# A written TensorE order for the chunked scans, low halves on VectorE, and one offset for all matmul operands

## The chip, the cores and the metric

One core of one Trainium2 chip runs the whole program. The metric is device time of one execution in microseconds (us). The kernel before was timed three times: 1361.96, 1358.02 and 1358.82 us, median 1358.82. TensorE is called PE, VectorE DVE (in code `V`), ScalarE ACT (`A`), GpSimd POOL (`G`), and SP is the engine whose queue issues nearly all DMAs.

## What is computed

The reference is an encoder of two layers on x of shape (1, 512, 1024) in float32. Cut to its bones:

```python
for layer in (0, 1):
    if layer == 0:  # one input projection for both kinds of heads
        q, k, v, z, xbc, dt = split(rms_norm(x) @ w_in)
        a = neighbourhood_attention(rms_norm(q), rms_norm(k), v, rel_bias)   # 8 heads of 64
        xs, B, C = split(silu(conv4(xbc)))                                   # 16 heads of 64, 4 groups
        y = ssd_scan(xs, dt, B, C) + flip(ssd_scan(flipped)) + D * xs        # 4 chunks of 128 tokens
        x = x + concat(a, group_rms_norm(y * silu(z))) @ w_out               # 1536 -> 1024
    else:
        x = x + grouped_query_attention(rotary(rms_norm(x) @ w_qkv)) @ w_o
    g, u = split(rms_norm(x) @ w13)                                          # hidden 2816
    x = x + (silu(g) * u) @ w2
```

Within a chunk of the scan, `y = ((C B^T) * decay) (x dt)`; between chunks a state of 128 x 64 per head is passed on, forward and backward.

## The kernel before

Activations are kept transposed: eight tiles of 128 channels by 512 tokens. Every large product is formed from three matmuls in fp32r, because each operand is split in a high half (rounded to fp32r) and a low half (the rest): `mm3` (L139 to L144) issues low weights by high activations (L142), high by low (L143) and high by high (L144). `load_w` (L130 to L137) brings 128 x 1024 raw weights by a DMA on SP's queue (L134), ACT copies the high half (L135), and DVE or POOL subtracts to get the low half (L136). `prep` (L160) splits activations the same way (high L162, low L163).

A block of projections is a generator of eight steps, each one `mm3`, so 24 matmuls of 128x512. `stream` loads the weights of a block one block ahead. In layer 0, 32 steps of query and key blocks come first; then `run(n)` threads the rest of those blocks and the six blocks of scan group 0 between the parts of the attention heads (`quota`, L664); step 96 calls `dt_path`, which works out the time steps and their cumulated decays.

Then the loop at L689 goes over the four groups of the scan. It drains the stream of the group's six blocks `g{g}_{i}` (two gates, B, C and two x blocks, each of the last four with a convolution of three DVE operations, L507) and writes down `ssd_group(g)` (L538 to L660) as one piece. Its matmuls, in the order of the program: four transposes `bt` and eight `xt`, the products `cb` of B and C, the states `st` from `xw` (x times dt-weights; forward half on DVE, backward half on POOL, L566), then for two head pairs the products `yd` of `xtok` with the masked decays `cf` (worked out head by head by ACT, DVE and POOL, L597 to L625), and `yo` from the passed states `H` (L583, L586). Adding up, gating and a group norm (`gs`, L649 to L660) follow; the result is split into `so..xh`, `so..xl`. The tile scheduler decides how PE interleaves a group's small matmuls with the next group's projections; nothing in the code fixes it. The low halves of the weights of groups 1 to 3 and of the output projection (L703, 16 loads of 640 columns) are worked out by POOL. The output projection `oA` (L697 to L706) and the last two scan tiles' share (`tail`, bank `t`) end the mixer. The sum of squares for the norm of each FFN is added up on POOL (`sumsq`, L720; `f_acc`, L173), while DVE works out `f_xl` (L163).

PSUM banks are handed out by tag (`bank`, L81): `p` two and `x` one for projections, `s` two, `t` two, `c` one for the scan. SBUF tiles come from pools in the order in which they are opened; in the built program the weights, `xg`, `x` and `s` tiles start at byte addresses that are 480 modulo 512, and the tiles of the lanes opened by a layer's part (`early`, `mix`, `grp`, `n`, `nb`, the `hh`/`hl` of the FFN, the attention's tiles) at 448 modulo 512.

Of the kernel before, what the change touches and what calls it, by code (L numbers as in the profile page):

```python
# [37 lines left out]
W2_SPLIT = (8, 8, 6)  # L38
NSLOT = 12
PB, HLB = 6, 4  # L40
WARM = 10
# [23 lines left out]
def encoder_kernel(ctx: ExitStack, tc: tile.TileContext, xt, vec, cst, rope, nab, w_v, w_qk, w_dt, w_ssd,  # L65
# [38 lines left out]
    def f(ap):  # L104
        return ap.bitcast(F32)
# [24 lines left out]
    def load_w(src, cols, name, eng=None):  # L130
        hi = wsp.tile([P, 1024], F32R, name=f"{name}_h", tag="wh", bufs=WH)
        lo = wsp.tile([P, 1024], F32R, name=f"{name}_l", tag="wl", bufs=WL)
        raw = wsp.tile([P, 1024], F32, name=f"{name}_r", tag="wr", bufs=WR)[:, 0:cols]
        nc.sync.dma_start(raw, src)  # L134
        A.activation(hi[:, 0:cols], raw, AF.Copy)  # L135
        (eng or V).tensor_tensor(lo[:, 0:cols], raw, f(hi)[:, 0:cols], ALU.subtract)  # L136
        return hi, lo  # L137
# [69 lines left out]
    def even_mixer(lp):  # L207
# [5 lines left out]
        A.preload_act_table_set(LNEXP)  # L213
        zt = small("zt", P, 1)
        V.memset(zt, 0.0)
# [6 lines left out]
        for n in range(2):  # L222
            t = lp.tile([P, 6, S], F32R, name=f"early{n}", tag="grp", bufs=2)
            early += [t[:, i] for i in range(6)]
# [285 lines left out]
        def ssd_blocks(g):  # L510
            gt = lp.tile([P, 6, S], F32, name=f"grp{g}", tag="grp", bufs=2)
            conv_cols = (8 + g, 12 + g, 2 * g, 2 * g + 1)

            def matmuls(w, i):
                ps = bank(f"g{g}_{i}")
                for k in range(KB):
                    mm3(ps, w, k * P, xn[k], ALL, k == 0, k == KB - 1)
                    yield
                if i > 3:
                    A.activation(gt[:, i], ps, AF.Copy)  # L520
                else:
                    conv(ps, conv_cols[i], gt[:, i])
                if i == 3:
                    si = A.activation(gt, gt, AF.Silu)
# [13 lines left out]
        def ssd_group(g, gt):  # L538
# [7 lines left out]
            for i in range(2):  # L546
                ps = bank(f"xt{g}_{i}", "t")
# [3 lines left out]
                A.activation(t, ps, AF.Copy)  # L551
                xtok.append(t)
            ps = bank(f"cb{g}", "t")
            for c in range(NCH):
# [7 lines left out]
            for d in range(2):  # L562
                for i in range(2):
                    t = xslot(f"xw{g}_{d}_{i}")
                    h0 = d * 16 + g * RG + 2 * i
                    (V if d == 0 else G).tensor_tensor(t.rearrange("p (c h e) -> p c h e", c=NCH, h=2),  # L566
                                    xtok[i].rearrange("p (c h e) -> p c h e", c=NCH, h=2),
                                    d3v(wst)[:, :, h0:h0 + 2].unsqueeze(3).to_broadcast([P, NCH, 2, HD]), ALU.mult)
                    xw.append(t)
            H = lane(f"H{g}", "hs", 1, cols=3 * S).rearrange("p (n d h e) -> p n d h e", n=3, d=2, h=RG)  # L570
            for n in range(3):
                sps = bank(f"st{g}_{n}", "s")
                for d in range(2):
# [12 lines left out]
                V.tensor_tensor(H[:, n], H[:, n], s5, ALU.add)  # L586

            ys = []
            for i in range(2):
                yd = bank(f"yd{g}_{i}", "c")  # L590
                es = []
                for hh in range(2):
# [32 lines left out]
                    V.tensor_tensor(e, e, m, ALU.mult)  # L625
                    es.append(e)
                for c in range(NCH):
                    for hh, e in enumerate(es):
                        T.matmul(yd[64 * hh:64 * hh + 64, c * P:(c + 1) * P],
                                 xtok[i][:, c * P + hh * 64:c * P + hh * 64 + 64], e[:, c * P:(c + 1) * P],  # L630
                                 start=True, stop=True)
# [16 lines left out]
                ys.append(y)  # L648
            gs = bank(f"gs{g}", "s")  # L649
# [4 lines left out]
            sum_rows(gs, sqs[0], f"gs{g}")  # L654
            r = rsqrt_wide(gs, 1.0 / 256, f"gn{g}")
# [5 lines left out]

        blocks = [t for b in range(4) for t in qk_blocks(b)] + list(ssd_blocks(0))
        fill = stream(blocks, 1)
        quota = (12, 12, 10, 10, 8, 8, 6, 6, 6, 6)  # L664
        steps = [0]

        def run(n):
            for _ in range(n):
                next(fill, None)
                steps[0] += 1  # L670
                if steps[0] == 96:
                    dt_path()

        run(32)
        for i in range(10):
            n = quota[i]
            cuts = (0, (n + 2) // 3, (2 * n + 2) // 3, n)
# [19 lines left out]
        for k in range(KB):  # L697
            res[k] = xslot(f"xr{k}")
            nc.sync.dma_start(res[k], xt[k])
        for o in range(KB):  # L700
            ps = bank(f"oA{o}")
            for k, n in ((0, 5), (5, 5)):
                w = load_w(w_o0[o, :, k * P:(k + n) * P], n * P, f"wo{o}_{k}", G)  # L703
                for kk in range(n):
                    mm3(ps, w, kk * P, mix[k + kk], ALL, k + kk == 0, k + kk == 9)
            V.tensor_tensor(res[o], res[o], ps, ALU.add)  # L706
        tail(w_t0, mix[10:], "t0")
# [11 lines left out]

    def sumsq(name):  # L720
        acc = None
        for k in range(KB):
            acc = accsq(acc, res[k], name, G)
        return acc

    def ffn(layer, gname, hp):
# [9 lines left out]
        for i in range(HB):  # L736
# [429 lines left out]
```

## Time and profile before

| | us |
|---|---|
| median of three runs | 1358.82 |
| the profiled execution, its own time | 1357.06 |
| its span, first to last instruction | 1355.3 |
| PE busy in the span | 1311.6 |
| DVE busy | 806.6 |
| ACT busy | 606.4 |
| POOL busy | 267.4 |
| first matmul of group 0's states (`st`) | 169.2 |
| first matmul of FFN 0 | 401.1 |

The profiled execution is 1.76 us below the median. The mean granted clock of TensorE was 0.992 of full speed. Busy times of PE rest on modelled ends; the spacing of starts is what a row of equal matmuls really takes.

### The profile page before, as it was taken

The numbers are of one execution on the slowest core, as the hardware profiler recorded it, in microseconds if no ns is written. First come the engines' busy times: TensorE is split into PE (matmuls) and PEld (weight loads), VectorE is DVE, ScalarE is ACT, GpSimd is POOL, SyncE is SP. The second block draws the span as 40 slices with busy tenths as digits, with TensorE's granted clock in tenths as the row PEclk, the third lists the DMA queues.
The fourth block names the chain that finished last, engine by engine and source line by source line (L and its number), as shares of the span: only waits on it lengthen the run. The fifth ranks groups of instructions, "written<-read, shape, count | busy, mean of one in ns | idle before, by whom it ended". The sixth has DMA issues, their size and how long they took to land.

```text
span 1355.3 us, 16780 instructions
## 1 busy us (share of the span) xinstructions
PE 1311.6 (97%) x6278; PEld 1067.1 (79%) x6278; DVE 806.6 (60%) x1210; ACT 606.4 (45%) x1028; POOL 267.4 (20%) x240
## 2 busy tenths in 40 slices
PE   9999988989999999999999999999999999999998
PEld 7777776767777888888888878778878888888886
DVE  6788697887766444444323377998874444443221
ACT  6675566566444233222222347777653222332220
POOL 4013344343340000000000135655230000000000
PEclk9999999989999999999999999999999999999999
DMA  6344343434433332333333334321123233233331
GB/s 232 94 118 141 88 148 95 139 98 132 125 97 110 103 99 93 93 101 113 89 99 89 104 103 100 105 58 40 47 94 94 93 99 104 94 94 102 104 116 52
DMA packets 49761, 138.82 MB, mean 102 GB/s; under 512 B 6736, under 2 KB 6864, under 8 KB 49680
## 3 DMA queue, kind: packets, MB, share of 16 engines
q1 hardware_dynamic: 49392, 137.23, 33.3%
q8 instruction: 49, 0.80, 0.2%
q10 hardware_dynamic: 288, 0.52, 0.1%
q14 instruction: 32, 0.26, 0.1%
HBM read 127.11 MB, written 2.23 MB: 95 GB/s over the span
## 4 chain that ended last, share of the span: by engine, by line
PE 77%; DVE 14%; ACT 5%; issue 3%; DMA 1%; POOL 0%; SPq 0%; DVEq 0%; ACTq 0%; POOLq 0%
PE fo L144 6%; PE fo L142 6%; PE fo L143 6%; PE fu L144 6%; PE fu L142 6%; PE fu L143 6%; PE fg L143 6%; PE fg L144 6%; PE fg L142 6%; PE vps L260 2%; PE g L144 1%; PE g L142 1%; PE g L143 1%; PE opt L921 1%; DVE f_xl L163 1%
## 5 line engine op out<-in xcount | busy, mean ns | idle before, releaser
L143 PE MATMUL fg<-f_xl,wfg_h 128*128 128x512 f32 x352 | 137.1, 390 | 3.9 <-DVE f_xl L163 3.9
L142 PE MATMUL fo<-hh,wf_l 128*128 128x512 f32 x352 | 139.2, 396 | 0.0
L143 PE MATMUL fo<-hl,wf_h 128*128 128x512 f32 x352 | 139.2, 396 | 0.0
L144 PE MATMUL fo<-hh,wf_h 128*128 128x512 f32 x352 | 139.2, 396 | 0.0
L144 PE MATMUL fg<-f_xh,wfg_h 128*128 128x512 f32 x352 | 136.9, 389 | 0.0
L142 PE MATMUL fu<-f_xh,wfu_l 128*128 128x512 f32 x352 | 136.9, 389 | 0.0
L144 PE MATMUL fu<-f_xh,wfu_h 128*128 128x512 f32 x352 | 136.9, 389 | 0.0
L143 PE MATMUL fu<-f_xl,wfu_h 128*128 128x512 f32 x352 | 136.9, 389 | 0.0
L142 PE MATMUL fg<-f_xh,wfg_l 128*128 128x512 f32 x352 | 136.9, 389 | 0.0
L135 ACT ACTIVATE wf_h<-wf_r 128x1024 fp32r<-128x1024 f32 (+1 forms) x48 | 47.5, 989 | 186.5 <-PE fo L144 164.4
L136 DVE TENSOR_TENSOR wf_l<-wf_r,wf_h 128x1024 fp32r<-128x1024 f32 (+1 forms) x48 | 54.5, 1136 | 126.7 <-ACT wf_h L135 126.7
L135 ACT ACTIVATE wfg_h<-wfg_r 128x1024 fp32r<-128x1024 f32 x44 | 46.7, 1060 | 149.6 <-issue 131.2
L135 ACT ACTIVATE wfu_h<-wfu_r 128x1024 fp32r<-128x1024 f32 x44 | 46.7, 1061 | 130.6 <-PE fg L144 130.1
L745 DVE TENSOR_TENSOR g<-fu,fr_r 128x512 f32<-128x512 f32 x44 | 30.4, 691 | 124.3 <-PE fu L144 123.1
L743 DVE TENSOR_TENSOR g<-fg,fr_r 128x512 f32<-128x512 f32 x44 | 30.2, 691 | 88.2 <-PE fg L144 88.1
L143 PEld LDWEIGHTS fg<-f_xl,wfg_h 128*128 128x128 f32 x352 | 66.1, 188 | 18.6 <-DVE f_xl L163 4.8
L173 POOL TENSOR_TENSOR o_acc<-o_acc,o_sq 128x512 f32<-128x512 f32 x7 | 10.8, 1538 | 350.6 <-ACT o_sq L172 350.6
L144 PEld LDWEIGHTS fo<-hh,wf_h 128*128 128x128 f32 x352 | 66.1, 188 | 16.1
L143 PEld LDWEIGHTS fo<-hl,wf_h 128*128 128x128 f32 x352 | 66.1, 188 | 15.9
L142 PEld LDWEIGHTS fo<-hh,wf_l 128*128 128x128 f32 x352 | 66.1, 188 | 15.9
L142 PE MATMUL g<-n_xh,w_l 128*128 128x512 f32 x192 | 78.3, 408 | 0.0
L144 PE MATMUL g<-n_xh,w_h 128*128 128x512 f32 x192 | 78.1, 407 | 0.0
(415 smaller groups left out, 3153.6 us busy)
## 6 DMA issues: line engine op xcount, KB each, us to landing
wfg_r<-in_w_fa SPq DMA_DIRECT2D x44, 512.0 KB, 3.5
wfu_r<-in_w_fa SPq DMA_DIRECT2D x44, 512.0 KB, 3.5
wf_r<-in_w_fb SPq DMA_DIRECT2D x32, 512.0 KB, 3.5
w_r<-in_w_ssd SPq DMA_DIRECT2D x24, 512.0 KB, 3.6
wf_r<-in_w_fb SPq DMA_DIRECT2D x16, 384.0 KB, 3.1
wo_r<-in_w_o SPq DMA_DIRECT2D x16, 320.0 KB, 2.9
nb<-in_nab SPq DMA_DIRECT2D x16, 256.0 KB, 3.0
ec<-ecumd SPq DMA_DIRECT2D x32, 128.0 KB, 3.5
```

Source lines behind the costliest of these rows:

```text
L135: A.activation(hi[:, 0:cols], raw, AF.Copy)
L136: (eng or V).tensor_tensor(lo[:, 0:cols], raw, f(hi)[:, 0:cols], ALU.subtract)
L142: T.matmul(ps, wl[:, a], xh[:, b], start=first, stop=False)
L143: T.matmul(ps, wh[:, a], xl[:, b], start=False, stop=False)
L144: T.matmul(ps, wh[:, a], xh[:, b], start=False, stop=last)
L163: V.scalar_tensor_tensor(lo, xt, g, f(hi), ALU.mult, ALU.subtract)
L173: eng.tensor_tensor(acc, acc, sq, ALU.add)
L260: T.matmul(vps[t], x_, w_[:, ws_], start=k + n == 0, stop=k == KB - 1 and n == 2)
L743: V.tensor_tensor(g, gp, rstd, ALU.mult)
L745: V.tensor_tensor(g, up, rstd, ALU.mult)
L921: T.transpose(pt[:, a * 256 + n * P:a * 256 + (n + 1) * P], pr[n][:, (2 * kp + a) * P:(2 * kp + a + 1) * P], ident)
```

## The change

It has four parts.

**A written PE order.** Inside `tc.manual_schedule(engines={PE})` PE runs in program order. `ssd_group` becomes a generator that stops at five places, and between them `run` takes a fixed number of steps (`SSD_QUOTA`) out of one continuous stream: all projection blocks of all groups, and behind them the output projection. Each group starts `LEAD` steps behind the end of its own projections. The group norm is split off (`ssd_norm`) and runs `NORM_LAG` steps later. The output projection goes in trios of blocks: the eight k-blocks from attention and the first two groups for each block of the trio, then the next two k-blocks for all three. Banks of the scan move (`cb` from `t` to `s`, and so on) and `grp` has three buffers.

**Low halves off POOL.** All low halves of weights in the scan, the backward `xw` and the FFNs' sums of squares move to DVE. POOL keeps `mb` and `cb` of the heads.

**One offset.** A dummy tile of 544 bytes replaces `zt` (512 bytes) in the pool `sm`; all tiles of the layers' parts then start at 480 modulo 512, as the weights do.

**Room.** The DMA scratch shrinks from 16384 to 2048 bytes, which makes room for the third `grp`.

Line numbers shift: the matmuls of `mm3` are L153 to L155, the low half L147, `bt` L553, `xt` L560, `cb` L566, `xw` L577, `st` L589, `yd` L643, `yo` L656, `gs` L680 and L681.

```diff
+LEAD = (12, 12, 12, 0)
+SSD_QUOTA = ((10, 8, 10, 2, 12), (10, 8, 10, 2, 12), (10, 8, 10, 2, 12), (10, 8, 10, 2, 12))
+NORM_LAG = (12, 12, 6, 14)
+SHIFT = 136
...
+    V.memset(sm.tile([P, SHIFT], F32, name="shift", tag="shift", bufs=1)[:, 0:1], 0.0)
...
-        zt = small("zt", P, 1)
+        zt = lane("zt", "nb", 2)[:, 0:P]
...
-                yield (lambda i=i: load_w(w_ssd[g * 6 + i], 1024, f"w{g}_{i}", V if g == 0 else G)), lambda w, i=i: matmuls(w, i)
+                yield (lambda i=i: load_w(w_ssd[g * 6 + i], 1024, f"w{g}_{i}", V)), lambda w, i=i: matmuls(w, i)
...
-                    (V if d == 0 else G).tensor_tensor(t.rearrange("p (c h e) -> p c h e", c=NCH, h=2),
+                    V.tensor_tensor(t.rearrange("p (c h e) -> p c h e", c=NCH, h=2),
...
+        def out_blocks():
+            for trio in (range(3), range(3, 6), range(6, KB)):
+                ps = {}
+                for o in trio:
+                    ps[o] = bank(f"oA{o}")
+                    w = load_w(w_o0[o, :, 0:8 * P], 8 * P, f"wo{o}", V)
+                    for k in range(8):
+                        mm3(ps[o], w, k * P, (ctx_n + ssd_out)[k], ALL, k == 0, False)
+                        yield
+                w = load_w([w_o0[o, :, 8 * P:10 * P] for o in trio], 256 * len(trio), f"wq{trio[0]}", V)
...
+        def both():
+            yield from stream(blocks, 1)
+            yield from out_blocks()
...
-        for g in range(SSD_G):
-            if g:
-                fill = stream(list(ssd_blocks(g)), 1)
+        with tc.manual_schedule(engines={mybir.EngineType.PE}):
+            for g in range(SSD_G):
+                while steps[0] < 64 + 48 * (g + 1) + LEAD[g]:
+                    run(1)
+                for at in ssd_group(g, ready[g]):
+                    run(SSD_QUOTA[g][at])
+                norm = ssd_norm(g)
+                next(norm)
+                later.append((steps[0] + NORM_LAG[g], norm))
+            while later:
+                run(1)
             for _ in fill:
                 pass
-            ssd_group(g, ready[g])
...
-                rstd = bcast_rstd(sumsq(f"f{layer}"), f"fr{layer}")
+                rstd = bcast_rstd(sumsq(f"f{layer}", V), f"fr{layer}")
```

PE, at the start of group 0's scan, before (the number behind a letter and `_` is the group; `g1_5` is a projection of group 1, `cb0`, `st0` and `xw0` belong to the scan of group 0):

```order
L555 MATMUL cb0_1693<-grp0_390 128x128 x4
L577 MATMUL st0_0_1711<-xw0_0_0_1702,btok0_1677 128x128
L577 MATMUL st0_1_1717<-xw0_0_0_1702,btok0_1677 128x128
L142 MATMUL g1_5_1956<-n7_xh_945,w1_5_l_1919 128x512
L577 MATMUL st0_0_1711<-xw0_0_1_1704,btok0_1677 128x128
L577 MATMUL st0_0_1711<-xw0_1_0_1706,btok0_1677 128x128
L577 MATMUL st0_0_1711<-xw0_1_1_1708,btok0_1677 128x128
L577 MATMUL st0_1_1717<-xw0_0_1_1704,btok0_1677 128x128
L577 MATMUL st0_1_1717<-xw0_1_0_1706,btok0_1677 128x128
L577 MATMUL st0_1_1717<-xw0_1_1_1708,btok0_1677 128x128
L143 MATMUL g1_5_1956<-n7_xl_946,w1_5_h_1918 128x512
```

The states followed the products `cb0` at once, with single matmuls of the projection between them. The same place now, behind ten steps (30 matmuls) of `g1_5` and `g1_0` that follow `cb0`:

```order
L153 MATMUL g1_0_1793<-n5_xh_735,w1_0_l_1718 128x512
L154 MATMUL g1_0_1793<-n5_xl_736,w1_0_h_1717 128x512
L155 MATMUL g1_0_1793<-n5_xh_735,w1_0_h_1717 128x512
L589 MATMUL st0_0_1813<-xw0_0_0_1766,btok0_1741 128x128
L589 MATMUL st0_0_1813<-xw0_0_1_1768,btok0_1741 128x128
L589 MATMUL st0_0_1813<-xw0_1_0_1770,btok0_1741 128x128
L589 MATMUL st0_0_1813<-xw0_1_1_1772,btok0_1741 128x128
L589 MATMUL st0_1_1819<-xw0_0_0_1766,btok0_1741 128x128
L589 MATMUL st0_1_1819<-xw0_0_1_1768,btok0_1741 128x128
L589 MATMUL st0_1_1819<-xw0_1_0_1770,btok0_1741 128x128
L589 MATMUL st0_1_1819<-xw0_1_1_1772,btok0_1741 128x128
```

The twelve matmuls of the states stand in one piece, and 30 matmuls lie between `cb0` and them.

POOL, from the scan of group 0 on, before (`w1_2_l` is the low half of a weight of group 1, `w2_4_l` of group 2):

```order
L566 TENSOR_TENSOR xw0_1_0_1706<-xtok0_0_1684,wst_385 128x512
L566 TENSOR_TENSOR xw0_1_1_1708<-xtok0_1_1691,wst_385 128x512
L608 TENSOR_TENSOR cb1_1757<-cb1_1757,cum_383 128x512
L606 TENSOR_TENSOR mb2_1811<-cbg0_1699,dt_382 128x512
L136 TENSOR_TENSOR w1_2_l_2018<-w1_2_r_2019,w1_2_h_2017 128x1024
L606 TENSOR_TENSOR mb3_1833<-cbg0_1699,dt_382 128x512
L608 TENSOR_TENSOR cb3_1830<-cb3_1830,cum_383 128x512
L136 TENSOR_TENSOR w1_3_l_2053<-w1_3_r_2054,w1_3_h_2052 128x1024
```

The same engine now:

```order
L621 TENSOR_TENSOR cb1_1894<-cb1_1894,cum_385 128x512
L619 TENSOR_TENSOR mb2_2006<-cbg0_1763,dt_384 128x512
L621 TENSOR_TENSOR cb3_2025<-cb3_2025,cum_385 128x512
L619 TENSOR_TENSOR mb3_2028<-cbg0_1763,dt_384 128x512
L621 TENSOR_TENSOR cb5_2339<-cb5_2339,cum_385 128x512
L619 TENSOR_TENSOR mb6_2451<-cbg1_2183,dt_384 128x512
```

Only four operations per group (two `cb`, two `mb`) remain on POOL; the `xw` and the low halves stand in DVE's row instead.

More of the change, by code (lines that the diff above doesn't have):

```diff
@@ L133, in load_w @@
         raw = wsp.tile([P, 1024], F32, name=f"{name}_r", tag="wr", bufs=WR)[:, 0:cols]
-        nc.sync.dma_start(raw, src)
+        parts = src if isinstance(src, list) else [src]
+        for n, part in enumerate(parts):
+            w = cols // len(parts)
+            nc.sync.dma_start(raw[:, n * w:(n + 1) * w], part)
         A.activation(hi[:, 0:cols], raw, AF.Copy)
@@ L222, in even_mixer @@
         for n in range(2):
-            t = lp.tile([P, 6, S], F32R, name=f"early{n}", tag="grp", bufs=2)
+            t = lp.tile([P, 6, S], F32R, name=f"early{n}", tag="grp", bufs=3)
             early += [t[:, i] for i in range(6)]
@@ L626, in ssd_group @@
                     es.append(e)
+                yield 2 + 2 * i
                 for c in range(NCH):
@@ L648, in ssd_group, with ssd_norm @@
                 ys.append(y)
-            gs = bank(f"gs{g}", "s")
+                if i == 0:
+                    yield 3
+            ssd_y[g] = ys
+        ssd_y = {}
+        def ssd_norm(g):
+            ys = ssd_y[g]
             sqs = [slot(f"gsq{g}_{i}") for i in range(2)]
@@ L660, in ssd_group @@
                                           mixslot if g < 3 else xgslot)
[L662 to L665, printed above, removed]
+        def out_blocks():
[6 more added lines that the diff above has]
+                        mm3(ps[o], w, k * P, (ctx_n + ssd_out)[k], ALL, k == 0, False)
+                        yield
+                w = load_w([w_o0[o, :, 8 * P:10 * P] for o in trio], 256 * len(trio), f"wq{trio[0]}", V)
+                for n, o in enumerate(trio):
+                    res[o] = xslot(f"xr{o}")
+                    nc.sync.dma_start(res[o], xt[o])
+                    for k in range(2):
+                        mm3(ps[o], w, (2 * n + k) * P, ssd_out[4 + k], ALL, False, k == 1)
+                        yield
+                    V.tensor_tensor(res[o], res[o], ps[o], ALU.add)
+        blocks = [t for b in range(4) for t in qk_blocks(b)] + [t for g in range(SSD_G) for t in ssd_blocks(g)]
+        def both():
+            yield from stream(blocks, 1)
+            yield from out_blocks()
+        fill = both()
+        steps, later = [0], []
         def run(n):
@@ L670, in run @@
                 steps[0] += 1
-                if steps[0] == 96:
+                if steps[0] == DT_STEP:
                     dt_path()
+                if later and steps[0] >= later[0][0]:
+                    next(later.pop(0)[1], None)
         run(32)
         for i in range(10):
-            n = quota[i]
+            n = NA_QUOTA[i]
             cuts = (0, (n + 2) // 3, (2 * n + 2) // 3, n)
```

36 lines of the change are left out of this document (18 added, 18 removed).

## The prediction

> **What bounds the kernel now.** I read the page first, then the windows, the waits, and the groups of each engine for the stage that the change rewrites. The page's chain says who ends last:
>
> ```profile
> PE 77%; DVE 14%; ACT 5%; issue 3%; DMA 1%; POOL 0%; SPq 0%; DVEq 0%; ACTq 0%; POOLq 0%
> ```
>
> TensorE carries the kernel, so time can come from two places alone: from PE standing idle, and from matmuls that take longer than they need. The windows from group 0's states (169) to the first FFN matmul (401) show the first (columns: window, length, busy time and count of PE, weight loads, DVE, ACT, POOL, then granted clock, DMA share, GB/s):
>
> ```profile
> 169.00:224.00 55.00, 48.20 (x258) 39.05 (x256) 45.22 (x70) 35.68 (x69) 22.01 (x13) 0.97 0.35 113
> 224.00:276.00 52.00, 46.12 (x247) 36.32 (x245) 42.62 (x64) 33.38 (x64) 20.95 (x12) 1.00 0.42 132
> 276.00:330.00 54.00, 49.13 (x247) 38.14 (x245) 44.81 (x66) 34.32 (x66) 22.56 (x15) 0.94 0.43 121
> 169.00:401.00 232.00, 209.99 (x1067) 166.19 (x1066) 182.44 (x269) 138.29 (x264) 94.99 (x57) 0.98 0.40 122
> ```
>
> PE is idle for 232.0 - 210.0 = 22.0 us, and the clock costs 55 x 0.03 + 54 x 0.06 = 4.9 us more. DVE is busy for 182 of 232 us, so it is the engine to watch. The waits of PE in this stage:
>
> ```profile
> PE yo L642 <- DVE H L586: 6.2, 5, 2.2
> PE bt L542 <- ACT grp L524: 4.4, 2, 3.2
> PE st L577 <- DVE xw L566: 4.0, 5, 1.4
> PE yd L629 <- DVE cf L625: 3.4, 5, 0.9
> PE gs L127 <- DVE gs_ql L126: 2.5, 3, 1.5
> ```
>
> These 20.5 us are nearly all of the idle time. Each is a small matmul that the scheduler put ahead of a projection too early: PE runs in order, and what stands behind cannot pass. 16.1 of them wait for DVE.
>
> **The written order.** What PE must do does not change much. Order counts 675 matmuls of 128x512 between `cb0` and the first FFN matmul before and 684 after (144, 144, 126 and 270 in the four groups). Their spacing is read off the FFN's start, where nothing waits: 21 steps from the first row to the second, 4.76 us, 0.2267 each.
>
> ```profile
> 401.10 0.39 PE L142 MATMUL fg<-f_xh,wfg_l 128*128 128x512 f32 x1
> ...
> 405.86 0.39 PE L142 MATMUL fg<-f_xh,wfg_l 128*128 128x512 f32 x1
> 408.23 0.50 PE L143 MATMUL fg<-f_xl,wfg_h 128*128 128x512 f32 x1 [1.98 <-DVE f_xl L163]
> ```
>
> So 232.1 us hold 675 x 0.2267 = 153.0 of projections, 1.6 for 240 `oA` matmuls that are 6.5 ns slower (below), 22.0 idle and 4.9 clock; the remaining 50.6 us, 12.6 per group, are the small matmuls and the changes between them. I keep 12.6, though single pieces instead of scattered ones may shorten it. PE then needs 32.6 + 12.6 = 45.2 us for groups 0 and 1, 41.2 for group 2, 73.8 for group 3.
>
> Between two of a group's parts now stand 2 to 12 steps, 1.4 to 8.2 us of PE work, while the longest wait above was 3.2 us. If DVE keeps pace, all five kinds of wait are covered. `yd` of the second head pair is the least covered: two steps stand before it.
>
> **What DVE gets and loses.** The rows of DVE in this stage, those that are slowed or that I price with:
>
> ```profile
> L507 DVE SCALAR_TENSOR_TENSOR grp<-g,vect,grp 128x511 f32<-128x511 f32 (+1 forms) x36 | 26.5, 739 | 0.9 <-ACT grp L504 0.9
> L614 DVE SCALAR_TENSOR_TENSOR m<-cbg,dt,m 128x128 f32<-128x128 f32 x32 | 19.2, 629 | 0.2
> L618 DVE SCALAR_TENSOR_TENSOR cf<-cb,cum,cf 128x128 f32<-128x128 f32 x31 | 16.9, 573 | 0.2 <-DMA cb<-cumd 0.2
> L625 DVE TENSOR_TENSOR cf<-cf,m 128x512 f32<-128x512 f32 x16 | 13.8, 863 | 1.3 <-ACT cf L624 1.3
> L566 DVE TENSOR_TENSOR xw<-xtok,wst 128x512 f32<-128x512 f32 x7 | 8.9, 1292 | 6.6 <-ACT xtok L551 6.6
> L189 DVE TENSOR_TENSOR gn_r<-gn_r,gn_t 128x512 f32<-128x512 f32 x4 | 8.5, 2124 | 0.0
> L645 DVE TENSOR_TENSOR ec<-yo,ec 128x384 f32<-128x384 f32 x16 | 8.3, 544 | 0.0
> L583 DVE TENSOR_TENSOR H<-H,dec 128x512 f32<-128x512 f32 x8 | 8.0, 1002 | 1.0 <-ACT H L581 1.0
> L126 DVE TENSOR_TENSOR gs_ql<-gsq,gs_qh 128x512 fp32r<-128x512 f32 x4 | 5.5, 1379 | 1.7 <-ACT gs_qh L125 1.7
> L647 DVE TENSOR_TENSOR y<-yd,grp 128x512 f32<-128x512 f32 x8 | 5.5, 682 | 0.0
> L136 DVE TENSOR_TENSOR wt_l<-wt_r,wt_h 128x1024 fp32r<-128x1024 f32 x2 | 2.5, 1225 | 2.7 <-ACT wt_h L135 2.7
> ```
>
> Equal shapes differ: a 128x512 operation takes 682 ns with an operand in PSUM (`y`) and up to 2124 ns with all in SBUF (`gn_r`). Undisturbed lengths, and how soon the next starts, stand in the timeline where POOL is idle:
>
> ```profile
> 172.51 0.33 DVE L618 SCALAR_TENSOR_TENSOR cf<-cb,cum,cf 128x128 f32<-128x128 f32 x1
> 172.78 0.34 DVE L614 SCALAR_TENSOR_TENSOR m<-cbg,dt,m 128x128 f32<-128x128 f32 x1
> 173.05 0.69 DVE L583 TENSOR_TENSOR H<-H,dec 128x512 f32<-128x512 f32 x1
> ```
>
> The excess over 0.34 and 0.682 us is 9.2 (`m`) + 7.2 (`cf`) + 2.9 (`cf,m`) + 4.3 (`xw`) + 5.8 (`gn_r`) + 2.6 (`H`) + 2.8 (`gs_ql`) = 34.8 us. It falls beside POOL's work:
>
> ```profile
> L136 POOL TENSOR_TENSOR w_l<-w_r,w_h 128x1024 fp32r<-128x1024 f32 x14 | 35.7, 2551 | 33.0 <-ACT w_h L135 31.1 <-issue 1.8
> L136 POOL TENSOR_TENSOR wo_l<-wo_r,wo_h 128x640 fp32r<-128x640 f32 x16 | 26.2, 1635 | 33.1 <-ACT wo_h L135 33.1
> L566 POOL TENSOR_TENSOR xw<-xtok,wst 128x512 f32<-128x512 f32 x8 | 10.9, 1374 | 27.2 <-ACT xtok L551 27.2
> L606 POOL TENSOR_TENSOR mb<-cbg,dt 128x512 f32<-128x512 f32 x8 | 10.3, 1286 | 18.1 <-PE yd L629 10.5 <-DVE cf L618 7.6
> L608 POOL TENSOR_TENSOR cb<-cb,cum 128x512 f32<-128x512 f32 x8 | 9.3, 1163 | 11.8 <-DMA cb<-cumd 9.2 <-DVE yd L646 1.6 <-DMA cf<-cumd 0.9
> ```
>
> 95.0 us of POOL cost DVE 34.8, so 0.37 per us. The first three rows go: 72.8 us of POOL, 27 us of DVE back. In return DVE takes the 14 low halves at 1.225 (17.2), eight of 1024 columns, two of 768 and one of 512 for the output projection (12.2, by columns) and eight `xw` (5.5): 34.9 us. DVE's load thus grows by about 8 us while the stage is to shrink, and in the middle groups that decides. Order puts 73 operations between the `cbl` of groups 1 and 2: 6 low halves (7.4), 12 of the convolution (8.9), 16 of 128x128 (5.4), 8 of 128x384 (4.4) and 31 of 128x512 at 0.685 (21.2), in all 47.3 us; POOL's 19.6/4 = 4.9 us in a group add 1.8: 49.1. The starts above lie 0.06 us and more closer than the lengths; 73 x 0.06 = 4.4 leaves 44.7 if DVE never waits. I take 47, midway, for groups 1 and 2, above PE's 45.2 and 41.2: there DVE sets the pace. Group 0 lacks the norm (68 operations) and stays under PE's 45.2; in group 3 DVE's 78 operations, some 55 us, lie beside 73.8 of PE.
>
> The start shifts too. Before, 189 projections of the scan ran ahead of `cb0` (169.2), now 180: 2.0 us earlier, and 192 query and key matmuls at 6.5 ns give 1.2. One wait there loses cover and another gains it:
>
> ```profile
> PE cps L477 <- DVE dtmp L474: 2.5, 1, 2.5
> ```
>
> Eight more matmuls stand ahead of `cps` (1.8 us of this covered), but the last head's `nctx` now follows its transposes at once, so that PE waits for their copies, up to two 0.7 us; I set the two against each other. `cb0` then ends at 166.0, the FFN starts at 166.0 + 45.2 + 47 + 47 + 73.8 = 379.0, and the stage gives 401.1 - 379.0 = 22.1 us.
>
> SP's queue loses its waits for POOL and gets the same for DVE's low halves; they are in the 47. The scratch's size and the third `grp` I cost at nothing: no DMA of the scan comes from POOL's queue, and a further buffer adds no wait; should the loads run later by it, the cover is the block that is loaded ahead, 5.4 us.
>
> **One offset.** Here the matmuls themselves get shorter. The page and the windows of an `fg`/`fu` stretch (all operands at 480) and an `fo` stretch (moving operand at 448):
>
> ```profile
> L142 PE MATMUL fo<-hh,wf_l 128*128 128x512 f32 x352 | 139.2, 396 | 0.0
> L142 PE MATMUL fu<-f_xh,wfu_l 128*128 128x512 f32 x352 | 136.9, 389 | 0.0
> ```
>
> ```profile
> 420.00:470.00 50.00, 50.00 (x222) 41.42 (x221) 25.32 (x32) 17.88 (x22) 0.00 (x0) 1.00 0.30 95
> 670.00:720.00 50.00, 50.00 (x216) 40.24 (x215) 15.51 (x16) 13.36 (x16) 4.64 (x3) 1.00 0.32 89
> ```
>
> In 50 us of a full PE go 222 against 216 matmuls, 6 to 7 ns each. It is not a matter of line or stage, since at the end of the same stage scan tiles in `mix` (448) and in `xg` (480) meet weights of the same pool:
>
> ```profile
> L143 PE MATMUL oA<-so_xl,wo_h 128*128 128x512 f32 x48 | 19.2, 399 | 0.0
> ...
> L143 PE MATMUL t<-so_xl,wt_h 128*128 128x512 f32 x16 | 6.2, 390 | 0.0
> ```
>
> Three `fo` lines give 3 x 2.3 = 6.9 us, and 144 matmuls of layer 1's output projection 0.9. The Trainium skill speaks against this: its page "TensorE: Matmul & The Clock Gate", Step-by-step: what each phase is for, gives TensorE two independent read ports, so that loading weights takes nothing from the running matmul, and a gap of 216 ns for 512 columns wherever the operands lie. By that rule this part is worth nothing; the trace does not agree, with 222 against 216.
>
> **FFN starts.** The row at 408.23 waits 1.98 us for `f_xl`, which POOL's sums `f_acc` slow. The sums now come behind the last `f_xl` on DVE: seven of 0.69, 4.8 us, beside 5.4 us of matmuls of the next block, while the broadcast stands four matmuls into that block and may wait about 1 us. I take 1.5 us for each of the two layers, 3.0, between 1.0 and 2.0 each.
>
> **Sum.** 22.1 + 6.9 + 0.9 + 3.0 = 32.9, so 1357.06 - 32.9 = 1324.2 for an execution like the profiled one, and with its 1.76 us below the median 1326.
>
> **The rivals.**
>
> *DVE sets the pace at full length.* If operations do not overlap, the middle groups cost 49.1 and some 2 of waits, 51, group 0 47 and group 3 75: the FFN starts at 390, and 11.1 us instead of 22.1 give 1337. The starts 0.27 apart for 0.33 long speak against it; that DVE now has some 200 us of lengths (43, 47.3, 47.3, 55 and 7 for POOL) in 213 speaks for it. The Trainium skill's page "VectorE: DVE Perf Modes", The DRAIN you can't avoid, has the next operation wait until the pipe is empty; by that rule this rival holds, and the rows at 172.51 and 172.78 do not agree. Chance 0.22.
>
> *The offset is not the cause.* Then 6.9, 0.9, 1.2 and 1.6 fall away, 10.6: 1337. The three pairs of rows speak against it, though all are correlations. Chance 0.13.
>
> *PE never waits.* The groups take 45.2, 45.2, 41.2 and 73.8, the FFN starts at 371.4, and the kernel comes to 1318; if standing in one piece also saves a seventh of the 12.6 us per group (assumed, no row shows it), 1311. For it: DVE before had 50 us of slack. Against it: 44.7 us is what DVE needs in a middle group without any wait. Chance 0.10.
>
> *Slower.* A written order cannot step aside. If DVE falls behind (a low half of 1.2 us ahead of `cf` in its row, a weight late behind it), each of the 32 hand-offs of the scan waits in full where the scheduler's order ran something else. Everything else gives 10.8 us, so the FFN must start after 401.1 + 10.8 + 4 = 416 to lose: 37 us over my 379, 1.2 us more at every hand-off. Before, 20 waits in all came to 20.5 us with far less between the parts. At 1.5 us each the kernel comes to 1326 + 48 = 1374. Chance 0.05.
>
> That the change does not happen can be left out: order and addresses are in the built program.
>
> **How the numbers follow.** My forecast has 0.42. The first two rivals together come to 1348 (0.04), hand-off waits short of the slower case to about 1359 (0.04), the third rival reaches down to 1311. The range 1312 to 1346 leaves out these two, the slower case and half of the third, 0.18. About 0.3% (4 us) is what a measurement can tell: faster than that 0.91, within 0.04, slower 0.05.
>
> **What would show it.** The first `fg` matmul near 379; groups of about 45, 47, 47 and 74 us between the `cb` products; PE idle from 166 to there under 12 us, no wait over 3 us, and the half clock gone from the scan; `m`, `cf` and `gn_r` near 0.34 and 0.7 us; `fo` at 389 to 390 ns and 222 matmuls in 50 us; the wait of 1.98 us gone. I am wrong if PE's waits for `cf`, `H` or `xw` still sum to 15 us, if SP waits long for DVE's `w_l`, or if `fo` stays at 396.

## The result, and the profile after

The changed kernel takes 1314.59 us (median of four runs, 1312.72 to 1315.06) against 1358.42 of the kernel before: ratio 0.9669, interval 0.965 to 0.9688. The profiled execution took 1314.37 us, span 1312.6, so 42.7 us less than the one of before. The forecast of 1326 was 11 us too high; the time lies at the low end of the range (1312 to 1346), where the rival stood that has PE never waiting (1318, or 1311).

Where the 42.7 us are, from the starts of the first matmuls of each stage in the two traces (us):

| mark | before | after | gained since the last mark |
|---|---|---|---|
| first `cb` of group 0 | 168.2 | 161.4 | 6.8 |
| `cb` of group 1 | 222.4 | 204.2 | 11.4 |
| `cb` of group 2 | 275.2 | 248.4 | 8.6 |
| `cb` of group 3 | 329.0 | 297.0 | 5.2 |
| first `fg`, layer 0 | 401.1 | 370.5 | -1.4 |
| first `fo`, layer 0 | 643.2 | 611.0 | 1.6 |
| last `fo`, layer 0 | 766.2 | 730.4 | 3.5 |
| first `fg`, layer 1 | 985.8 | 948.6 | 1.5 |
| first `fo`, layer 1 | 1227.8 | 1188.9 | 1.7 |
| end | 1355.3 | 1312.6 | 3.8 |

The projections moved between the groups: group 2 holds 126 of their matmuls now and held 142 before, group 3 holds 270 and held 240. The gain of 5.2 us for group 2 and the loss of 1.4 us for group 3 therefore belong together.

The page's chain of the changed kernel, to be held against the 77% of before:

```profile
PE 81%; DVE 12%; ACT 4%; issue 2%; DMA 1%; SPq 0%; POOL 0%; DVEq 0%; ACTq 0%; POOLq 0%
```

The windows of the changed kernel, one per group and one for the whole scan (same columns as before):

```profile
161.40:204.20 42.80, 42.80 (x247) 36.14 (x246) 38.97 (x68) 29.87 (x60) 6.20 (x4) 1.00 0.47 145
204.20:248.40 44.20, 43.87 (x249) 36.73 (x248) 43.11 (x73) 32.47 (x63) 6.58 (x4) 1.00 0.41 130
248.40:297.00 48.60, 42.79 (x230) 34.91 (x229) 41.78 (x72) 35.12 (x66) 4.78 (x4) 0.93 0.38 119
297.00:370.50 73.50, 72.29 (x364) 58.94 (x363) 59.00 (x94) 40.81 (x76) 7.28 (x4) 1.00 0.46 145
```

```profile
161.40:370.50 209.10, 201.75 (x1082) 166.72 (x1081) 182.86 (x306) 138.27 (x262) 24.83 (x16) 0.98 0.44 136
```

PE is busy without a gap in group 0 and all but 0.3 us of group 1; 7.4 us of idle time are left where 22.0 were, 5.8 of them in group 2, with the clock at 0.93 there: behind the longest wait the clock was at half for 6.8 us. DVE is as busy as before (182.9 against 182.4 us) in 23 us less time: 43.1 of 44.2 us in group 1. The largest waits of PE in the changed kernel (from 140 to 400 us):

```profile
PE oA L153 <- ACT cf L629: 4.6, 1, 4.6
PE yd L643 <- DVE cf L638: 1.1, 2, 0.8
PE oA L154 <- DVE so_xl L174: 0.6, 2, 0.3
PE oA L153 <- ACT so_xh L173: 0.5, 1, 0.5
PE fr_ss L135 <- DVE fr_ql L134: 0.3, 1, 0.3
```

The waits for `H`, `xw`, `grp` and `gs_ql` are gone, and so are those for `cps` and `f_xl`. The first row names ACT, but its `cf` (284.4) cannot hold a product of the output projection. The timelines of ACT and DVE have what does, the two halves of its weight:

```profile
267.12 1.05 ACT L146 ACTIVATE wo_h<-wo_r 128x1024 fp32r<-128x1024 f32 x1
```

```profile
284.36 1.22 DVE L147 TENSOR_TENSOR wo_l<-wo_r,wo_h 128x1024 fp32r<-128x1024 f32 x1
```

PE's `oA` starts at 285.72. The high half had been ready since 268.2: the low half stood in DVE's row behind the scan's operations for 16 us. On DVE the lengths fell as forecast (`cf,m` 685 against 863 ns, `gn_r` 749 against 2124, `m` 346 against 629):

```profile
L631 DVE SCALAR_TENSOR_TENSOR cf<-cb,cum,cf 128x128 f32<-128x128 f32 x32 | 11.6, 405 | 0.3 <-ACT cf L629 0.3
L638 DVE TENSOR_TENSOR cf<-cf,m 128x512 f32<-128x512 f32 x16 | 11.0, 685 | 0.9 <-ACT cf L637 0.9
L577 DVE TENSOR_TENSOR xw<-xtok,wst 128x512 f32<-128x512 f32 x16 | 10.1, 686 | 0.4 <-ACT xtok L562 0.4
L627 DVE SCALAR_TENSOR_TENSOR m<-cbg,dt,m 128x128 f32<-128x128 f32 x32 | 9.4, 346 | 0.0
L200 DVE TENSOR_TENSOR gn_r<-gn_r,gn_t 128x512 f32<-128x512 f32 x4 | 3.0, 749 | 0.0
```

Some excess stayed: `cf` 405 ns, `H` 790, `yn` 823, and one operation of the norm rose (`gn_t` at L199, 848 against 422). POOL's own operations beside the fuller DVE take longer too (`mb` 1692 against 1286 ns, `cb` 1430 against 1163). The second product of the FFNs, from the page:

```profile
L153 PE MATMUL fo<-hh,wf_l 128*128 128x512 f32 x352 | 136.9, 389 | 0.0
```

Most of the signs that the prediction named are there: the first `fg` comes even sooner than 379, the idle time is under 12 us, `fo` is at 389 ns with 222 matmuls in 50 us, the wait of 1.98 us is gone, and of the waits for `cf`, `H` and `xw` 1.1 us are left. SP's queue waits 35.6 us for DVE's `w_l` where it waited 93.8 for POOL's. Two signs failed: one wait is longer than 3 us (4.6), and the half clock is not gone from the scan. Whether the reasons hold is another matter: three parts came at once, and the trace cannot tell which removed the waits.

### The profile page after: what moved, and what is told of

It reads as the page before. It is cut to its first block, busy times and chain, and to the rows that moved or that the text cites. A ratio compares the mean times of both kernels' runs of the same rounds, so it can differ in the third digit from the quotient of the medians.

```text
span 1312.6 us, 16744 instructions
## 1 busy us (share of the span) xinstructions
PE 1288.4 (98%) x6278; PEld 1062.6 (81%) x6278; DVE 805.2 (61%) x1262; ACT 604.0 (46%) x1023; POOL 167.5 (13%) x184
## 4 chain that ended last, share of the span: by engine, by line
PE 81%; DVE 12%; ACT 4%; issue 2%; DMA 1%; SPq 0%; POOL 0%; DVEq 0%; ACTq 0%; POOLq 0%
PE fo L155 6%; PE fo L154 6%; PE fo L153 6%; PE fu L153 6%; PE fu L155 6%; PE fu L154 6%; PE fg L155 6%; PE fg L154 6%; PE fg L153 6%; PE g L153 2%; PE g L154 2%; PE g L155 2%; PE vps L271 2%; PE opt L968 1%; PE oA L153 1%
## 5 line engine op out<-in xcount | busy, mean ns | idle before, releaser
L155 PE MATMUL fg<-f_xh,wfg_h 128*128 128x512 f32 x352 | 137.0, 389 | 0.0
L153 PE MATMUL fu<-f_xh,wfu_l 128*128 128x512 f32 x352 | 136.9, 389 | 0.0
L155 PE MATMUL fu<-f_xh,wfu_h 128*128 128x512 f32 x352 | 136.9, 389 | 0.0
L153 PE MATMUL fo<-hh,wf_l 128*128 128x512 f32 x352 | 136.9, 389 | 0.0
L155 PE MATMUL fo<-hh,wf_h 128*128 128x512 f32 x352 | 136.9, 389 | 0.0
L153 PE MATMUL fg<-f_xh,wfg_l 128*128 128x512 f32 x352 | 136.9, 389 | 0.0
L147 DVE TENSOR_TENSOR wf_l<-wf_r,wf_h 128x1024 fp32r<-128x1024 f32 (+1 forms) x48 | 54.5, 1136 | 122.2 <-ACT wf_h L146 122.2
L155 PEld LDWEIGHTS fg<-f_xh,wfg_h 128*128 128x128 f32 x352 | 66.2, 188 | 13.9
L154 PEld LDWEIGHTS fu<-f_xl,wfu_h 128*128 128x128 f32 x352 | 66.2, 188 | 13.7
L153 PEld LDWEIGHTS fu<-f_xh,wfu_l 128*128 128x128 f32 x352 | 66.1, 188 | 13.7
L153 PEld LDWEIGHTS fo<-hh,wf_l 128*128 128x128 f32 x352 | 66.1, 188 | 13.7
L155 PEld LDWEIGHTS fu<-f_xh,wfu_h 128*128 128x128 f32 x352 | 66.0, 188 | 13.7
```

The lines of the kernel that those rows point to most:

```text
L153: T.matmul(ps, wl[:, a], xh[:, b], start=first, stop=False)
L154: T.matmul(ps, wh[:, a], xl[:, b], start=False, stop=False)
L155: T.matmul(ps, wh[:, a], xh[:, b], start=False, stop=last)
```

## The experiments

Each median is followed by the ratio to the kernel before, run on the same chip, with its interval.

**The offset alone.** The first run adds it to the kernel before, the second takes it from the changed kernel.

```diff
 # b_offset, on the kernel before
+    V.memset(sm.tile([P, 8], F32, name="shift", tag="shift", bufs=1)[:, 0:1], 0.0)
 # a_offset448, on the changed kernel
-SHIFT = 136
+SHIFT = 128
```

> The kernel before with one pad of 32 bytes, so that all tiles of the layers' parts start at 480 modulo 512 like the weights; nothing else is changed. If unequal offsets lengthen a 512-column matmul by 6.5 ns (the prediction's term): fo rows 389 instead of 396 ns, both FFNs 6.9 us shorter, and with oA (1.6), queries and keys (1.2) and layer 1's output projection (0.9) about 1348 us against 1358.4. If the offset is not the cause: fo stays at 396 ns and the time at 1358.

> The changed kernel with the dummy tile at 512 instead of 544 bytes, so that the tiles of the layers' parts stand at 448 again; order and engines as in the change. Offset theory: fo back at 396 ns, each FFN's second product 3.5 us longer, about 1324 to 1325 us against 1314.6. Rival (the order made room for it): 1314.6, fo at 389 ns.

Measured: 1350.11 us, ratio 0.9941 (0.9926 to 0.9957), and 1324.35, ratio 0.9756 (0.9738 to 0.9774). By the medians the offset is worth 8.9 us alone and 9.8 us in the changed kernel (forecast 10.6); by the ratios, which hold each kernel against the one before on its own chip, it is 8.0 and 11.8, so the size is known to 2 to 4 us. The `fo` row of the changed kernel without the offset is that of before to the digit:

```profile
L153 PE MATMUL fo<-hh,wf_l 128*128 128x512 f32 x352 | 139.2, 396 | 0.0
```

and with the offset alone it is that of the changed kernel:

```profile
L143 PE MATMUL fo<-hh,wf_l 128*128 128x512 f32 x352 | 136.9, 389 | 0.0
```

The offset is the cause; the rival that it is not has fallen.

**Is it 448, or unequal offsets?** One run moves everything to 448, one puts the FFN's halves at four other distances from the weights.

```diff
 # a_all448: ahead of all pools
+    V.memset(kp.tile([P, 120], F32, name="pad")[:, 0:1], 0.0)
 # a_offsets: own tags for hh and hl, a pad ahead of each
+        pads = ((8, 8), (32, 32))[layer]      # floats
+            hi = hlane(f"hh{layer}_{i}", "hh", HB, F32R)
+            lo = hlane(f"hl{layer}_{i}", "hl", HB, F32R)
```

> The changed kernel with a pad of 480 bytes ahead of all pools, so that weights, xg, x, slots and the layers' tiles all start at 448 modulo 512. If equality of the two operands' offsets is what counts: 1314.6, all matmul rows at 389 ns. If 448 itself is slow: fg, fu, fo, g and oA all at 396 ns, some 4300 matmuls by 6.5 ns, 28 us, about 1343.

> The changed kernel with the FFN's high halves hh and low halves hl at other offsets than the weights' 480: layer 0 hh 32 and hl 64 bytes on, layer 1 hh 128 and hl 256 bytes on (0, 32, 96, 224 modulo 512). If any difference between moving operand and weights costs: all fo rows near 396 ns, time about 1322. If only 448 (32 below) does: all at 389, 1314.6. If it depends on the distance: rows that differ by layer and half.

Measured: 1314.34 us, ratio 0.9673 (0.9652 to 0.9694), and 1320.36 in one run. With all operands at 448 nothing is lost:

```profile
L154 PE MATMUL fo<-hh,wf_l 128*128 128x512 f32 x352 | 137.0, 389 | 0.0
```

So it is the two operands' addresses relative to each other. With the moving operand at other distances, the `fo` rows of layer 0 (`hh` 32, `hl` 64 bytes on) and of layer 1 (`hh` 128, `hl` 256 on):

```profile
L153 PE MATMUL fo<-hh,wf_l 128*128 128x512 f32 x176 | 70.0, 398 | 0.0
L154 PE MATMUL fo<-hl,wf_h 128*128 128x512 f32 x176 | 69.3, 394 | 0.0
L155 PE MATMUL fo<-hh,wf_h 128*128 128x512 f32 x176 | 69.3, 394 | 0.0
```

```profile
L153 PE MATMUL fo<-hh,wf_l 128*128 128x512 f32 x170 | 66.8, 393 | 0.0
L155 PE MATMUL fo<-hh,wf_h 128*128 128x512 f32 x169 | 66.1, 391 | 0.0
L154 PE MATMUL fo<-hl,wf_h 128*128 128x512 f32 x169 | 65.6, 388 | 0.0
```

Against 389 ns the price depends on the distance: 5 to 9 ns at 32 and 64 bytes, 2 to 4 at 128, none at 256 (and 7 at 448, where the moving operand stands 32 bytes the other way). The three matmuls of an `mm3` are mixed in these rows with their neighbours' weight loads, so that a curve cannot be drawn from them, and what in the chip makes it was not tried.

**Off POOL alone, and back.** One run moves the low halves, the backward `xw` and the FFNs' sums to DVE in the kernel before; the other moves them back to POOL in the changed kernel.

```diff
 # b_dve (a_pool does the reverse, with G for group 1 on)
-                yield (lambda i=i: load_w(..., V if g == 0 else G)), ...
+                yield (lambda i=i: load_w(..., V)), ...
-                    (V if d == 0 else G).tensor_tensor(...)
+                    V.tensor_tensor(...)
-                w = load_w(w_o0[o, :, k * P:(k + n) * P], n * P, f"wo{o}_{k}", G)
+                w = load_w(w_o0[o, :, k * P:(k + n) * P], n * P, f"wo{o}_{k}", V)
-            acc = accsq(acc, res[k], name, G)
+            acc = accsq(acc, res[k], name, V)
```

> The kernel before with only the low halves of weights, the backward xw and the FFNs' sums of squares moved from POOL to DVE; PE order left to the scheduler, offsets as before. If the relief of DVE from POOL is a good part of the scan's gain: PE's 20.5 us of waits in the scan about halve, the two FFN starts give 3, about 1345 us. If the written order does it alone: the waits stay near 20 us and only the FFN starts gain, about 1355.

> The changed kernel with the low halves of groups 1 to 3 and of the output projection, the backward xw and the FFNs' sums back on POOL; written order and offset as in the change. If the written order needs a DVE that is not slowed: DVE's operations lengthen again by some 27 us in the scan, hand-offs wait in full, 1330 us or more. If the parts between the hand-offs cover that too: only the FFN starts lose 3.3 us, about 1318.

Measured: 1349.73 us, ratio 0.9946 (0.9924 to 0.9967), and 1342.49, ratio 0.9887 (0.9869 to 0.9906). Relief of DVE (it has more operations, but POOL no longer lengthens them) gains 9.2 us alone (7.3 by the ratio), between the two expectations; taking it away costs the changed kernel 27.9 (29.6 by the ratios). Of the 7.8 us between the traces of the first run and of the kernel before, 5.6 lie ahead of the scan: the first `cb` comes at 162.6 instead of 168.2. PE's wait of 2.5 us for `cps` is gone, and with it the stretch of 3.4 us at half clock behind it, which cost 1.7; the rest is another such stretch, at 79.8, which this execution did not have although the two kernels do the same up to there. The wait for `cps` came from POOL: beside a low half on POOL, one of DVE's operations for `cps` took 1.98 us, and without it 0.28 (the first two lines before, the third in this run):

```profile
138.95 2.39 POOL L136 TENSOR_TENSOR w_l<-w_r,w_h 128x1024 fp32r<-128x1024 f32 x1 [4.95 <-DVE dtmp L470]
139.51 1.98 DVE L470 SCALAR_TENSOR_TENSOR dtmp<-dtmp 128x128 f32<-128x128 f32 x1
137.95 0.28 DVE L470 SCALAR_TENSOR_TENSOR dtmp<-dtmp 128x128 f32<-128x128 f32 x1
```

The two FFN starts give 1.7 and 1.2 us. The scan itself gained nothing: from the first `cb` to the first `fg` it takes 234.0 us against 232.9. In the scan of that kernel other waits took the places:

```profile
PE yd L629 <- DVE y L647: 10.9, 3, 4.4
PE g L142 <- DVE w_l L136: 3.7, 4, 1.5
PE yd L629 <- DVE cf L625: 3.1, 4, 2.2
PE oA L142 <- DVE wo_l L136: 1.6, 1, 1.6
PE yo L642 <- DVE H L586: 1.0, 4, 0.4
```

```profile
162.60:396.60 234.00, 212.89 (x1078) 170.11 (x1077) 186.14 (x310) 139.73 (x266) 20.61 (x16) 0.95 0.41 119
```

`H` and `xw` hardly hold PE any more, but the single bank of `yd` does, and the clock is 0.95 on average over 234 us, 12 us lost. The changed kernel with POOL's work back has the lengths of before (`m` 781 ns, `cf,m` 871): from the first `cb` to the first `fg` DVE does 272 operations instead of 306 and is busy longer (188.2 against 182.9 us). PE idles as long as in the kernel before (22.2 us against 22.0), and the wait for `cps` is back:

```profile
PE yd L643 <- DVE cf L638: 8.9, 4, 3.1
PE bt L553 <- ACT grp L535: 6.5, 1, 6.5
PE yd L643 <- DVE y L661: 2.7, 3, 2.1
PE cps L488 <- DVE dtmp L485: 2.5, 1, 2.5
PE oA L153 <- DVE xr L705: 2.5, 1, 2.5
PE fg L154 <- DVE f_xl L174: 2.0, 1, 2.0
```

**The written order.** Three runs: the changed kernel with the scheduler free to place PE; with each group in one piece and the scheduler free; and with each group in one piece and PE's order written.

```diff
 # a_free, a_lump_free
-        with tc.manual_schedule(engines={mybir.EngineType.PE}):
+        if True:
 # a_lump_free, a_lump_written
+LEAD = (12, 12, 12, 1)
+SSD_QUOTA = ((0, 0, 0, 0, 0),) * 4
+NORM_LAG = (0, 0, 0, 0)
```

> The changed kernel without the manual schedule: same program order of the code, same engines and offsets, but the scheduler places PE's instructions. If the written order is what removes the waits: PE waits some 15 to 20 us in the scan again, about 1332 us. If the gain came from DVE's relief, the third grp buffer and the output projection spread into the last scan: within 4 us of 1314.6.

> The changed kernel without the manual schedule and with no projection steps between a group's parts (SSD_QUOTA all 0, NORM_LAG 0, group 3 one step behind its projections), so the code again writes each group in one piece and the scheduler places PE; low halves on DVE, offset, banks, stream and third grp as in the change. If the steps written between the parts are what the scheduler needs (they also order DVE): PE waits 15 to 25 us again in the scan, 1332 to 1342. If the stream, the banks and the third grp are enough: within 4 us of the 1316.8 without the manual schedule.

> As the run before, but with the manual schedule: PE runs each group's matmuls in one piece, with no projection between them. If hand-offs cost what no matmul covers (8 a group at 1 to 5 us each): 20 us or more per group, 1390 or more. If DVE is far enough ahead of PE for the order not to matter: 1315 to 1320.

Measured: 1316.78 us, ratio 0.9687 (0.966 to 0.9713); 1336.88, ratio 0.9854 (0.9838 to 0.9871); 1410.18, ratio 1.0389 (1.0371 to 1.0407). My theory for the first fell: without the manual schedule the median is 2 us higher, and the intervals do not tell that from nothing. The waits that were to return, 15 to 20 us, are 6.8 us in the scan:

```profile
PE oA L153 <- ACT so_xh L173: 2.4, 1, 2.4
PE oA L153 <- DVE wo_l L147: 2.3, 2, 2.0
PE yd L643 <- DVE cf L638: 1.6, 1, 1.6
PE g L153 <- DVE w_l L147: 0.5, 1, 0.5
```

The second run says what does count. The same kernel, scheduler free, with no steps between a group's parts in the code (the delay of the norm goes with them) is 20 us slower, and its waits are back, 19.8 us in all, the largest:

```profile
PE g L153 <- DVE w_l L147: 5.6, 3, 2.0
PE st L589 <- DVE xw L577: 3.4, 7, 0.7
PE oA L153 <- DVE wo_l L147: 3.0, 1, 3.0
PE yd L643 <- DVE y L661: 3.0, 1, 3.0
PE yd L643 <- DVE cf L638: 2.2, 1, 2.2
```

These are waits for low halves as much as for scan results. As I read the two runs, the scheduler ranks the operations of all engines by their place in the code: where a group is written in one piece, its DVE operations stand ahead of the low halves that the next projections need. The trace has such a place: the high half of a weight of the next group is ready at 222.4, its low half starts on DVE at 231.1, behind the operations of the scan, and PE waits for it until 232.4. The waits are measured; that the ranking is their reason is not shown. The third run shows what a written order costs without steps between: the first three groups take 68.3 to 69.3 us instead of 42.8 to 48.6, at a clock of 0.86 over the scan:

```profile
160.50:463.60 303.10, 233.29 (x1082) 192.76 (x1081) 192.46 (x306) 142.54 (x262) 21.41 (x16) 0.86 0.31 94
```

**The wait that is left.** Two runs load the output projection's weights one block ahead; the second also starts group 3 eight steps later.

```diff
-            yield from stream(blocks, 1)
-            yield from out_blocks()
+            yield from stream(blocks + list(out_blocks()), 1)   # out_blocks as (load, matmuls) pairs
 # a_ahead_lead
-LEAD = (12, 12, 12, 0)
+LEAD = (12, 12, 12, 8)
```

> The changed kernel with the output projection's blocks in the same stream as the projections, so that each weight is loaded and split one block ahead. The largest wait left in the scan is the first oA matmul for its low half, which DVE does late: 4.6 us, with 6.8 us at half clock behind it. If it goes: 4.6 + 3.4 = 8 us, about 1307. If DVE only pushes something else back: new waits of the same sum, 1313 to 1315.

> The changed kernel with the output projection's weights one block ahead and group 3 eight steps behind its projections instead of none. The run with the weights ahead lost its 4.6 us wait for wo_l but waited 4.2 us for group 3's silu and 2.9 us more for cf. If eight steps (5.4 us) cover the silu: 1309 to 1311. If the wait goes elsewhere again, because DVE is full there: 1313 to 1315.

Measured: 1313.89 us, ratio 0.9671 (0.965 to 0.9693), and 1312.07, ratio 0.9669 (0.9655 to 0.9683). Neither can be told from the change. The wait for `wo_l` went, and with the first run others of the same size came, as its second expectation had it:

```profile
PE bt L553 <- ACT grp L535: 4.2, 1, 4.2
PE yd L643 <- DVE cf L638: 2.9, 3, 1.4
PE oA L153 <- ACT so_xh L173: 1.5, 1, 1.5
```

In the trace of the first run DVE's last convolution for group 3 starts at 288.2 and the silu behind it at 290.6, against 287.9 and 290.0 in the changed kernel: DVE's row is no sooner done, so PE, which no longer waits for `wo_l`, waits there for the silu that `bt` needs. With the later start the median lies between the two expectations. The first `fg` comes at 368.0 instead of 370.5, a gain of 2.5 us in the scan; layer 1's mixer is 1.5 us longer in this trace, with two stretches of half clock (758.5 and 867.7) that the trace of the change lacks, and the ratio is that of the change.

**Is DVE full?** The last run gives DVE the rest of POOL's scan work.

```diff
-                        G.tensor_tensor(c4(mb), c4(cbg), per_chunk(d3v(dt)), ALU.mult)
+                        V.tensor_tensor(c4(mb), c4(cbg), per_chunk(d3v(dt)), ALU.mult)
-                        G.tensor_tensor(c4(cbk), c4(cbk), per_chunk(d3v(cum)), ALU.subtract)
+                        V.tensor_tensor(c4(cbk), c4(cbk), per_chunk(d3v(cum)), ALU.subtract)
```

> The changed kernel with the last 16 scan operations of POOL (mb and cb of the heads) on DVE as well. In group 1 DVE is busy 43.1 of 44.2 us while PE is busy 43.9. Four more operations of 0.685 us, starting 0.06 to 0.09 sooner than their length, are 2.4 us a group, less what POOL took from DVE (at most 1.8 by the prediction's 0.37 per us). If DVE is as full as that reads: 0.6 to 2.4 us in each of three groups, 1316 to 1322. If DVE still has slack, or POOL costs it more than the operations do: 1314.6 or less.

Measured: 1318.04 us, ratio 0.969 (0.9677 to 0.9703), in the range of the full DVE, though its interval overlaps that of the change. Group 1 grew to 51.3 us, with a `yd` wait of 4.4 us and the half clock behind it, while group 2 shrank to 45.2:

```profile
204.80:256.10 51.30, 46.31 (x249) 39.01 (x248) 46.01 (x80) 36.51 (x69) 0.00 (x0) 0.93 0.39 124
```

## Why the prediction was right, and where its steps failed

**What bounds it.** Right: the gain came from PE's waits and from the lengths of its matmuls. From the first `cb` to the first `fg` the stage is 23.8 us shorter. With 0.2267 us for each projection that is 14.7 less idle time, 9.5 less for the small matmuls and the changes between them (1.6 of it the offset of `oA`), 1.7 less at half clock, and 2.0 more for nine more projections.

**The written order, 22.1 us for the stage.** The stage gave 30.6 with the start, and the cause was misjudged in part. "If DVE keeps pace, all five kinds of wait are covered" held as far as the 2 to 12 steps between the parts go. The step that failed is the one before it: that the waits come from the scheduler's choice for PE, so that PE's order has to be written. With the scheduler free (`a_free`) the waits are 6.8 us and not 20.5, and the order that was written by hand adds nothing that the runs can show. What removes the waits is two things together: the steps written between the parts, which order DVE and the loads too, and a DVE without POOL beside it. Four kernels that all have the offset show it (medians, us):

| | POOL keeps its work | POOL's work on DVE |
|---|---|---|
| no steps between the parts | 1350.1 (`b_offset`) | 1336.9 (`a_lump_free`) |
| steps between the parts | 1342.5 (`a_pool`) | 1314.6 (the change; `a_free` 1316.8) |

The steps without relief gain 8 us and relief without the steps 13; together they gain 36, 15 more than the sum. `a_pool` and the change also have PE's order written, and all but `b_offset` have the third `grp`, the other banks, the one stream and the trios of the output projection. No run takes these away alone, so what they are worth stays open.

**The sizes within the stage.** Three terms were too dear. The start: I let the wait for `cps` be replaced by one for the last head's copies; it went without replacement, together with the half clock behind it, so `cb` came 6.8 us earlier and not 3.2. It went with POOL's work and not by the eight matmuls that now stand ahead of it: `a_pool` has them and waits 2.5 us. The small matmuls: 12.6 us per group held the cost of scattering them. The stage has 396 of them in both traces, but 37 changes between them and the projections instead of 83; with the parts whole, what is neither projection (at 0.2267) nor idle came to 42.8 - 32.6 = 10.2 us in group 0, 11.3 in group 1 and 73.5 - 61.2 - 1.2 = 11.1 in group 3. DVE's pace: I took 47 us midway between 44.7 and 49.1; group 1 took 44.2, with PE busy 43.9 and DVE 43.1. So the group took a little less than the lower bound of 44.7, and DVE and PE ended level. Group 2 (48.6 against 47) is the one that came out slower, by the 4.6 us wait for `wo_l`, a low half behind the scan in DVE's row, and the 3.4 us that the half clock behind it cost; that place I had named only in the slower rival. That the first `fg` at 370.5 so nearly meets the 371.4 of the rival that has PE never waiting is luck: the first `cb` came sooner and three groups were shorter than there, and group 2 was 7.4 us longer, with PE waiting.

**DVE at full length.** This rival has fallen. In group 1 the lengths of DVE's 73 operations add up to 49.1 us, just what the prediction had, and they were done in 43.1 us of busy time. In group 3 the prediction counted too few operations, 78 of some 55 us; the trace has 93 with lengths of 64.8 us, which the 73.5 us of PE covered. The rule of the Trainium skill's page "VectorE: DVE Perf Modes", The DRAIN you can't avoid, by which each would wait for an empty pipe, does not fit these rows; the same paragraph of the page excepts instructions that are not held, which start earlier, and the prediction left that out.

**One offset.** Right in mechanism and nearly in size: 8.9 and 9.8 us by the medians against 10.6. `fo` gave 7.0 of the 6.9 forecast. The query and key part gave 0.6 to 0.7 us (57.9 and 58.0 us from the first `qps` to the last `kps` in `a_ahead` and `a_lump_written`, at 480; 58.6 in `a_offset448` and `b_dve`, at 448; the other kernels have a stretch of half clock there) and not 1.2. Layer 1's mixer became 1.5 us shorter against 0.9, but before it held a stretch of 3.4 us at half clock at 905.8, so the 0.9 cannot be seen by itself. The two read ports that the Trainium skill's page "TensorE: Matmul & The Clock Gate", Step-by-step: what each phase is for, gives to TensorE do not exclude this effect: the four kernels above show it. That the gap holds "wherever the operands lie" is the prediction's reading of that section, which gives it by the columns.

**FFN starts, 3.0 us.** Right: 1.6 and 1.7 us.

**Slower.** The mechanism is real, with its place as described: without steps between, the written order makes the kernel 3.9% slower than before. The quotas of 2 to 12 steps are what kept the change on the other side.

## What to carry to other kernels

When several engines feed PE, first write the code so that filler work stands between the dependent parts, and look at what the scheduler does with it, before an order is written by hand; here the hand-written order showed no value of its own, and a large price where the hand-offs were not covered. A helper engine's cost can be what it does to the engine that works beside it: here some 72 us of POOL, for which PE waited 1.1 us in the kernel before, held back 28 us in the kernel with the steps. In a long run of matmuls compare the rows of equal shape: 396 against 389 ns was worth 10 us for one pad of 32 bytes.

## What was not expected of the hardware

- The distance between the addresses of the moving operand and the weights sets a matmul's time: 389 ns at equal offsets modulo 512, be they 480 or 448, 394 to 398 at 32 or 64 bytes, 391 to 393 at 128, 388 at 256. Why is not known.
- A wait of 2 to 5 us on PE was often followed by one or two stretches of 3.41 us at half clock (before: 143.7 and 144.6), but not always: the wait of 2.0 us for `f_xl` drew one in each layer in the run with the offset alone (405.1 and 988.8) and none in the profiled execution before. Such a stretch costs 1.7 us, so that a wait can cost nearly twice its length: PE's waits in the scan of `b_dve` took 21 us and the clock 12 more.
